# Weighted sum of two expert outputs: another row layout in HBM, hand-placed waits, and two VectorE instructions per tile

## The chip, the cores and the metric

The kernel runs on one core of one Trainium2 chip. The metric is the device time in microseconds (us) of one execution. The time before the change is 241.46 us, the median of 13 runs that lie between 241.12 and 242.02.

## The reference

A mixture-of-experts layer has sent each token to two experts, and the two results are combined with two weights per token. There are 16 x 1024 = 16384 tokens, two results of 512 float32 numbers for each, and 16384 x 2 weights.

```python
def reference(expert_outputs, combine_weights):      # (16,1024,2,512), (16,1024,2)
    weights = combine_weights[..., np.newaxis]
    return np.sum(expert_outputs * weights, axis=2).astype(np.float32)   # (16,1024,512)
```

67.1 MB are read and 33.5 MB are written; there are three arithmetic operations per output number.

## The kernel before, in words

The tokens are numbered through, and partition p of the 128 holds the 128 tokens from 128 p on. In HBM a partition's inputs are then 512 KB apart, its outputs 256 KB, and its weights 1 KB. The loop over `g` takes J = 8 tokens of every partition at a time, so there are 16 tiles. A tile is one load of 4 MB (32 KB in each partition, one contiguous run), one store of 2 MB (16 KB in each partition), and arithmetic between them.

Loads are issued by SyncE (L48) into `et`, which has four buffers; stores are issued by ScalarE (L66) from `ot`, which has four buffers too. The table of weights `wt` is one load of 128 KB, issued by ScalarE at the start (L43). A tile framework adds the semaphores: a load waits until VectorE has read the tile that used its buffer four tiles before; VectorE waits for the load, for the table, and for the store that used its output buffer four tiles before.

For each token i of the eight, VectorE runs two instructions. L57 multiplies the first expert's 512 numbers by the first weight into `ot`. L58 multiplies the second expert's 512 numbers by the second weight and adds what is in `ot`. The weight is a number per partition. These are 16 instructions a tile, on 128 x 512 elements each.

The last tile differs: the first product is made by ScalarE (L55, an activation that copies with a scale), and the store is cut in three, of 4, 2 and 2 tokens, each issued by ScalarE after its tokens are done. The first activation of a program needs a function table, which ScalarE loads in an instruction of its own.

All transfers run on the same 16 DMA engines. In the profile q1 is the queue that SyncE issues to, q10 the one that ScalarE issues to, and q14 carries instructions.

Of the kernel before, what the change touches and what calls it, by code (L numbers as in the profile page):

```python
# [1 line left out]

# [4 lines left out]


@with_exitstack
def kernel(  # L10
    ctx: ExitStack,
    tc: tile.TileContext,
    expert_outputs: bass.AP,
    combine_weights: bass.AP,
    out: bass.AP,
):


    nc = tc.nc
    b, s, k, h = expert_outputs.shape  # L20
    assert k == 2
    n = b * s
    P = nc.NUM_PARTITIONS
    per = n // P
    assert per * P == n
    eo = expert_outputs.rearrange("b s k h -> (b s) (k h)").rearrange("(p t) f -> p t f", p=P)
    cw = combine_weights.rearrange("b s k -> (b s) k").rearrange("(p t) k -> p (t k)", p=P)
    o = out.rearrange("b s h -> (b s) h").rearrange("(p t) f -> p t f", p=P)

    dt = mybir.dt.float32  # L30
    mult = mybir.AluOpType.mult
    add = mybir.AluOpType.add

    J = 8
    copy = mybir.ActivationFunctionType.Copy
    last = per // J - 1

    wpool = ctx.enter_context(tc.tile_pool(name="w", bufs=1))
    ipool = ctx.enter_context(tc.tile_pool(name="in", bufs=4))
    opool = ctx.enter_context(tc.tile_pool(name="out", bufs=4))  # L40

    wt = wpool.tile([P, per * k], dt)
    nc.scalar.dma_start(out=wt, in_=cw)  # L43

    for g in range(per // J):
        et = ipool.tile([P, J, k * h], dt)
        ot = opool.tile([P, J, h], dt)
        nc.sync.dma_start(out=et, in_=eo[:, g * J : (g + 1) * J, :])  # L48
        c0 = 0
        for c in (4, 2, 2) if g == last else (J,):  # L50
            for i in range(c0, c0 + c):
                t = g * J + i
                w0, w1 = wt[:, 2 * t : 2 * t + 1], wt[:, 2 * t + 1 : 2 * t + 2]
                if g == last:
                    nc.scalar.activation(out=ot[:, i, :], in_=et[:, i, 0:h], func=copy, scale=w0)  # L55
                else:
                    nc.vector.tensor_scalar_mul(out=ot[:, i, :], in0=et[:, i, 0:h], scalar1=w0)  # L57
                nc.vector.scalar_tensor_tensor(  # L58
                    out=ot[:, i, :],
                    in0=et[:, i, h : 2 * h],  # L60
                    scalar=w1,
                    in1=ot[:, i, :],
                    op0=mult,
                    op1=add,
                )
            nc.scalar.dma_start(  # L66
                out=o[:, g * J + c0 : g * J + c0 + c, :], in_=ot[:, c0 : c0 + c, :]
            )
            c0 += c


# [1 line left out]
_INS = ['expert_outputs', 'combine_weights']  # L73
_OUTS = [((16, 1024, 512), 'float32')]


# [23 lines left out]
```

## Time and profile before

| what | value |
|---|---|
| median of 13 runs | 241.46 us (241.12 to 242.02) |
| the profiled execution: time, span | 241.86 us, 240.1 us |
| DMA: mean rate over the span | 420 GB/s |
| HBM read, written | 67.24 MB, 33.55 MB |
| VectorE busy | 133.8 us (56%) |
| ScalarE busy | 6.4 us (3%) |
| first VectorE instruction | at 13.90 us |
| last store issued | at 236.53 us, landed 2.6 us later |

The span is the time from the first to the last instruction of the profiled execution. The time of that execution is 1.76 us longer than its span, for what lies around it. The profile is one execution, and it is 0.40 us above the median of the runs. "Landing" of a DMA is the moment its last semaphore signal arrives. In the page the DMA strip gives the busy share of the 16 DMA engines in 40 slices of 6.0 us each.

### The profile page before, as it was taken

The numbers are of one execution on the slowest core, as the hardware profiler recorded it, in microseconds if no ns is written. First come the engines' busy times: TensorE is split into PE (matmuls) and PEld (weight loads), VectorE is DVE, ScalarE is ACT, GpSimd is POOL, SyncE is SP. The second block draws the span as 40 slices with busy tenths as digits, with TensorE's granted clock in tenths as the row PEclk, the third lists the DMA queues.
The fourth block names the chain that finished last, engine by engine and source line by source line (L and its number), as shares of the span: only waits on it lengthen the run. The fifth ranks groups of instructions, "written<-read, shape, count | busy, mean of one in ns | idle before, by whom it ended". The sixth has DMA issues, their size and how long they took to land.

```text
span 240.1 us, 377 instructions
## 1 busy us (share of the span) xinstructions
DVE 133.8 (56%) x248; ACT 6.4 (3%) x9; POOL 0.2 (0%) x4
## 2 busy tenths in 40 slices
DVE  0068937629185490945819276391853918549062
ACT  0000000000000000000000000000000000000072
POOL 0000000000000000000000000000000000000000
DMA  7999999999999999999999999999999999999967
GB/s 268 439 434 431 388 407 459 414 420 459 426 429 434 442 407 431 453 418 448 442 426 426 426 437 426 423 453 437 435 437 415 431 426 442 420 442 439 412 289 306
DMA packets 5042, 100.81 MB, mean 420 GB/s; under 512 B 560, under 2 KB 688, under 8 KB 944
## 3 DMA queue, kind: packets, MB, share of 16 engines
q1 hardware_dynamic: 2304, 67.11, 65.3%
q10 hardware_dynamic: 2736, 33.69, 32.9%
q14 instruction: 2, 0.02, 0.0%
HBM read 67.24 MB, written 33.55 MB: 420 GB/s over the span
## 4 chain that ended last, share of the span: by engine, by line
DMA 56%; DVE 26%; another core or an unknown queue 13%; issue 1%; ACT 1%; SPq 0%; ACTq 0%; DVEq 0%
DMA et<-in_expert_outputs_dram 56%; DVE ot L58 16%; DVE ot L57 10%; ACT ot L55 1%; ACT L55 1%; SPq L48 0%; ACTq L66 0%; DVEq L95 0%; DVEq L57 0%; ACTq L55 0%
## 5 line engine op out<-in xcount | busy, mean ns | idle before, releaser
L57 DVE TENSOR_SCALAR ot<-et,wt 128x512 f32<-128x512 f32 x120 | 52.6, 480 | 93.4 <-DMA et<-in_expert_outputs_dram 79.5
L58 DVE SCALAR_TENSOR_TENSOR ot<-et,wt,ot 128x512 f32<-128x512 f32 x128 | 89.9, 745 | 9.3 <-ACT ot L55 9.3
L55 ACT ACT_TABLE_LOAD x1 | 1.3, 1283 | 227.8 <-DMA out_dram<-ot 227.8
L55 ACT ACTIVATE ot<-et,wt 128x512 f32<-128x512 f32 x8 | 5.1, 709 | 1.5 <-DVE ot L58 1.5
L84 POOL MEMSET const-bfloat16-1.0<- 128x1 bf16 x1 | 0.1, 103 | 0.0
L84 POOL MEMSET const-uint8-127<- 128x1 uint8 x1 | 0.1, 102 | 0.0
L84 POOL MEMSET const-float32-0.0<- 128x1 f32 x1 | 0.1, 100 | 0.2 <-issue 0.2
L84 POOL MEMSET const-float32-1.0<- 128x1 f32 x1 | 0.1, 99 | 0.0
## 6 DMA issues: line engine op xcount, KB each, us to landing
et<-in_expert_outputs_dram SPq DMA_DIRECT2D x16, 4096.0 KB, 49.5
out_dram<-ot ACTq DMA_DIRECT2D x15, 2048.0 KB, 24.8
out_dram<-ot ACTq DMA_DIRECT2D x1, 1024.0 KB, 3.9
out_dram<-ot ACTq DMA_DIRECT2D x2, 512.0 KB, 3.2
wt<-in_combine_weights_dram ACTq DMA_DIRECT2D x1, 128.0 KB, 13.1
```

What stands on the lines that cost most here:

```text
L55: nc.scalar.activation(out=ot[:, i, :], in_=et[:, i, 0:h], func=copy, scale=w0)
L57: nc.vector.tensor_scalar_mul(out=ot[:, i, :], in0=et[:, i, 0:h], scalar1=w0)
L58: nc.vector.scalar_tensor_tensor(out=ot[:, i, :], in0=et[:, i, h : 2 * h], scalar=w1, in1=ot[:, i, :], op0=mult, op1=add,)
L84: nc = _bacc.Bacc("TRN2", target_bir_lowering=False, num_devices=1)
```

## The change

Five things change together.

- The rows. The first 15360 tokens are dealt out 120 to a partition; the last 1024 tokens are a tile of their own, 8 to a partition. For the first 15 tiles a partition's inputs are then 480 KB apart in HBM and its outputs 240 KB. For the last tile they are 32 KB and 16 KB apart. The size of the runs that a DMA moves stays the same. The table of weights is loaded by two DMAs, of 240 and of 16 numbers per partition.
- The semaphores. They are placed by hand in one block. SyncE issues all loads in order. From the fifth on, a load waits for VectorE to have finished with the tile four before, as it did, and also for that tile's store to have landed. VectorE waits for both DMAs of the table, and then for each tile's load; it no longer waits for stores.
- VectorE's work on the first 15 tiles. One instruction multiplies the whole tile, 8192 numbers per partition, in place by its 16 weights, each repeated 512 times. A second one adds the two halves of each token, 4096 numbers per partition, into `ot`.
- ScalarE runs a one-element activation at its start, ahead of the two loads of the table. Its function table is loaded there.
- The last tile. ScalarE's product is written in place; VectorE's instruction is the same as L58. The store is cut in four, of two tokens each, and SyncE issues them.

The number of instructions on VectorE falls from 248 to 38. The number of DMAs and their bytes stay nearly the same.

```diff
@@ rows
-    eo = expert_outputs.rearrange("b s k h -> (b s) (k h)").rearrange("(p t) f -> p t f", p=P)
+    main = per - J
+    def rows(x):
+        a = x[0 : P * main, :].rearrange("(p t) f -> p t f", p=P)
+        b = x[P * main : n, :].rearrange("(p t) f -> p t f", p=P)
+        return lambda t, c: a[:, t : t + c, :] if t < main else b[:, t - main : t - main + c, :]
+    eo = rows(expert_outputs.rearrange("b s k h -> (b s) (k h)"))
...
@@ loads
-        nc.sync.dma_start(out=et, in_=eo[:, g * J : (g + 1) * J, :])
+    made = [2 * (g + 1) for g in range(G - 1)]
+        for g in range(G):
+            if g >= NOUT:
+                nc.sync.wait_ge(stored[g % NOUT], 16 * (g // NOUT))
+            ins = nc.sync.dma_start(out=et[:, g % NIN], in_=eo(g * J, J).rearrange("p j (k h) -> p j k h", k=k))
+            if g >= NIN:
+                ins._wait_ge(vec, made[g - NIN])
+            ins.then_inc(loaded[g], 16)
@@ table and stores
-    nc.scalar.dma_start(out=wt, in_=cw)
+        nc.scalar.activation(out=warm, in_=one, func=copy)
+        for t, c in ((0, main), (main, J)):
+            nc.scalar.dma_start(out=wt[:, t : t + c], in_=cw(t, c)).then_inc(weights, 16)
+        for g in range(G - 1):
+            nc.scalar.dma_start(out=o(g * J, J), in_=ot[:, g % NOUT])._wait_ge(
+                vec, made[g]).then_inc(stored[g % NOUT], 16)
@@ VectorE, first 15 tiles
-                    nc.vector.tensor_scalar_mul(out=ot[:, i, :], in0=et[:, i, 0:h], scalar1=w0)
-                nc.vector.scalar_tensor_tensor(out=ot[:, i, :], in0=et[:, i, h : 2 * h], scalar=w1,
-                    in1=ot[:, i, :], op0=mult, op1=add)
+        nc.vector.wait_ge(weights, 32)
+        for g in range(G - 1):
+            ek = et[:, g % NIN].rearrange("p j k h -> p (j k) h")
+            wb = wt[:, g * J : (g + 1) * J].rearrange("p j k -> p (j k)").unsqueeze(2)
+            nc.vector.tensor_tensor(out=ek, in0=ek, in1=wb.to_broadcast([P, J * k, h]), op=mult
+            )._wait_ge(loaded[g], 16).then_inc(vec, 1)
+            e = et[:, g % NIN]
+            nc.vector.tensor_tensor(out=ot[:, g % NOUT], in0=e[:, :, 0], in1=e[:, :, 1], op=add
+            )._wait_ge(vec, made[g] - 1).then_inc(vec, 1)
@@ last tile
-        for c in (4, 2, 2) if g == last else (J,):
+        for i in range(J):
...
+            if i % PIECE == PIECE - 1:          # PIECE = 2
+                f = i + 1 - PIECE
+                nc.sync.dma_start(out=o(g * J + f, PIECE), in_=ot[:, g % NOUT, f : i + 1]
+                )._wait_ge(vec, made[g - 1] + i + 1).then_inc(tail, 16)
```

More of the change, by code (lines that the diff above doesn't have):

```diff
@@ L25 @@
     assert per * P == n
-    eo = expert_outputs.rearrange("b s k h -> (b s) (k h)").rearrange("(p t) f -> p t f", p=P)
-    cw = combine_weights.rearrange("b s k -> (b s) k").rearrange("(p t) k -> p (t k)", p=P)
-    o = out.rearrange("b s h -> (b s) h").rearrange("(p t) f -> p t f", p=P)
+    J = 8
+    NIN = NOUT = 4
+    G = per // J
+    main = per - J
[4 more added lines that the diff above has]
+    eo = rows(expert_outputs.rearrange("b s k h -> (b s) (k h)"))
+    cw = rows(combine_weights.rearrange("b s k -> (b s) k"))
+    o = rows(out.rearrange("b s h -> (b s) h"))
     dt = mybir.dt.float32
@@ L32 @@
     add = mybir.AluOpType.add
-    J = 8
     copy = mybir.ActivationFunctionType.Copy
[L36 to L42, printed above, removed]
-    nc.scalar.dma_start(out=wt, in_=cw)
[L45 to L49, printed above, removed]
-        for c in (4, 2, 2) if g == last else (J,):
[L51 to L69, printed above, removed]
@@ new lines @@
+    pool = ctx.enter_context(tc.tile_pool(name="sbuf", bufs=1))
+    wt = pool.tile([P, per, k], dt)
+    warm = pool.tile([P, 1], dt)
+    et = pool.tile([P, NIN, J, k, h], dt)
+    ot = pool.tile([P, NOUT, J, h], dt)
+    loaded = [nc.alloc_semaphore(f"loaded{g}") for g in range(G)]
+    stored = [nc.alloc_semaphore(f"stored{i}") for i in range(NOUT)]
+    weights = nc.alloc_semaphore("weights")
+    tail = nc.alloc_semaphore("tail")
+    vec = nc.alloc_semaphore("vec")
+    act = nc.alloc_semaphore("act")
@@ new lines @@
+    one = nc.const_aps.tensor(1.0, (P, 1), dt)
+    PIECE = 2
+    made = [2 * (g + 1) for g in range(G - 1)]
+    with tc.tile_critical():
+        for g in range(G):
[10 more added lines that the diff above has]
+            nc.scalar.dma_start(out=o(g * J, J), in_=ot[:, g % NOUT])._wait_ge(
+                vec, made[g]
+            ).then_inc(stored[g % NOUT], 16)
+        nc.vector.wait_ge(weights, 32)
+        for g in range(G - 1):
+            ek = et[:, g % NIN].rearrange("p j k h -> p (j k) h")
+            wb = wt[:, g * J : (g + 1) * J].rearrange("p j k -> p (j k)").unsqueeze(2)
+            nc.vector.tensor_tensor(
+                out=ek, in0=ek, in1=wb.to_broadcast([P, J * k, h]), op=mult
+            )._wait_ge(loaded[g], 16).then_inc(vec, 1)
+            e = et[:, g % NIN]
+            nc.vector.tensor_tensor(
+                out=ot[:, g % NOUT], in0=e[:, :, 0], in1=e[:, :, 1], op=add
+            )._wait_ge(vec, made[g] - 1).then_inc(vec, 1)
+        g = G - 1
+        nc.scalar.wait_ge(weights, 32)
+        for i in range(J):
+            e, r = et[:, g % NIN, i], ot[:, g % NOUT, i]
+            w = wt[:, g * J + i]
+            ins = nc.scalar.activation(out=e[:, 0], in_=e[:, 0], func=copy, scale=w[:, 0:1])
+            if i == 0:
+                ins._wait_ge(loaded[g], 16)
+            ins.then_inc(act, 1)
+            nc.vector.scalar_tensor_tensor(
+                out=r, in0=e[:, 1], scalar=w[:, 1:2], in1=e[:, 0], op0=mult, op1=add
+            )._wait_ge(act, i + 1).then_inc(vec, 1)
+            if i % PIECE == PIECE - 1:
+                f = i + 1 - PIECE
+                nc.sync.dma_start(
+                    out=o(g * J + f, PIECE), in_=ot[:, g % NOUT, f : i + 1]
+                )._wait_ge(vec, made[g - 1] + i + 1).then_inc(tail, 16)
+        for i in range(NOUT):
+            nc.sync.wait_ge(stored[i], 16 * len(range(i, G - 1, NOUT)))
+        nc.sync.wait_ge(tail, 16 * (J // PIECE))
```

## The prediction

> **What bounds the kernel now.** I read the page first, then the busy time by stretches, the groups, the DMA issues, the waits of SyncE's queue and the timeline. The page's engine line, DMA strip and queue rows:
> ```profile
> DVE 133.8 (56%) x248; ACT 6.4 (3%) x9; POOL 0.2 (0%) x4
> DMA  7999999999999999999999999999999999999967
> DMA packets 5042, 100.81 MB, mean 420 GB/s; under 512 B 560, under 2 KB 688, under 8 KB 944
> q1 hardware_dynamic: 2304, 67.11, 65.3%
> q10 hardware_dynamic: 2736, 33.69, 32.9%
> q14 instruction: 2, 0.02, 0.0%
> ```
> The 16 DMA engines are full but for the first and the last slices; VectorE is busy 56%. Queue q1 holds the loads: 16 tiles x 128 rows of 32 KB are 2048 packets, and 16 signals per tile make 2304. 65.3% of 240.1 us is 156.8 us on each engine, over 128 rows: 1.22 us a row, 9.7 us a tile. A store of half the bytes is 4.85 us. The table is 688 - 560 = 128 packets, one a partition row.
>
> Busy time by stretches (us; DVE, ACT, POOL; clock; DMA share; GB/s):
> ```profile
> 4.00:14.00 10.00, 0.10 (x1) 0.00 (x0) 0.00 (x0) 1.00 1.01 432
> 24.00:38.00 14.00, 8.49 (x17) 0.00 (x0) 0.00 (x0) 1.00 0.99 406
> 125.00:154.00 29.00, 17.11 (x32) 0.00 (x0) 0.00 (x0) 1.00 1.01 433
> 228.00:232.00 4.00, 2.16 (x4) 3.99 (x6) 0.00 (x0) 1.00 0.85 365
> 232.00:236.00 4.00, 2.83 (x5) 2.21 (x4) 0.00 (x0) 1.00 0.66 271
> 236.00:240.00 4.00, 0.49 (x1) 0.00 (x0) 0.00 (x0) 1.00 0.65 261
> ```
> 432 to 433 GB/s is the same for loads alone and for loads with stores. So the middle is bound by bytes, 14.55 us a tile, and only idle DMA time can be won or lost. The one weak full stretch is 24 to 38. The idle is at the end: 0.15 x 4 + 0.34 x 4 + 0.35 x 4 = 3.4 us, of which some 1.3 us follow the last data.
>
> VectorE's two groups, then the two DMA issues that matter:
> ```profile
> L57 DVE TENSOR_SCALAR ot<-et,wt 128x512 f32<-128x512 f32 x120 | 52.6, 480 | 93.4 <-DMA et<-in_expert_outputs_dram 79.5
> L58 DVE SCALAR_TENSOR_TENSOR ot<-et,wt,ot 128x512 f32<-128x512 f32 x128 | 89.9, 745 | 9.3 <-ACT ot L55 9.3
> ```
> ```profile
> et<-in_expert_outputs_dram SPq DMA_DIRECT2D x16, 4096.0 KB, 49.5
> wt<-in_combine_weights_dram ACTq DMA_DIRECT2D x1, 128.0 KB, 13.1
> ```
> A 128 KB table that lands after 13.1 us, as late as the first tile of 4 MB (13.0 in the trace), says that each of its rows waits for a 32 KB row of the other queue. The waits of SyncE's queue:
> ```profile
> SPq L48 <- DVE ot L58: 102.8, 12, 8.6
> ```
> Today a load waits for VectorE alone. The timeline at tiles 11 to 13, and at the end:
> ```profile
> 168.73 0.88 DVE L57 TENSOR_SCALAR ot<-et,wt 128x512 f32<-128x512 f32 x2 [6.05 <-DMA et<-in_expert_outputs_dram]
> 184.14 0.88 DVE L57 TENSOR_SCALAR ot<-et,wt 128x512 f32<-128x512 f32 x2 [6.86 <-DMA et<-in_expert_outputs_dram]
> 198.69 0.88 DVE L57 TENSOR_SCALAR ot<-et,wt 128x512 f32<-128x512 f32 x2 [5.99 <-DMA et<-in_expert_outputs_dram]
> 227.79 1.28 ACT L55 ACT_TABLE_LOAD   x1 [227.79 <-DMA out_dram<-ot]
> 232.62 1.66 ACTq L66 DMA_DIRECT2D out_dram<-ot  x2
> 236.53 0.34 ACTq L66 DMA_DIRECT2D out_dram<-ot  x1
> ```
> One step is 15.41 us instead of 14.55, beside one of the two instruction fetches of q14. At the end ScalarE loads its table only when the last tile is there, and stands 1.46 us behind its own store issue.
>
> **The change part by part.** Sums go against the profiled execution: span 240.1, time 241.86, 0.40 above the median 241.46; I add the difference to the median.
>
> *VectorE.* A tile's 16 instructions become two, of 8192 and 4096 elements, both with two tensor inputs. The timeline gives starts 0.397 us apart for L57 and 0.661 for L58. From below: all elements at L57's pace, 24 x 0.397 = 9.5 us. From above: 24 pieces at L58's pace, 15.9 us. I take a fixed part and a slope: if L57 takes half a cycle per element and L58 a whole one, 745 - 480 = 265 ns are 256 cycles, so 1.035 ns per element and 0.215 us fixed; 8192 then cost 8.69, 4096 cost 4.45, together 13.2 us with the wait between them (now 8.5). That is under 14.55, so the DMA still hides it in the middle. The Trainium skill ("VectorE: DVE Perf Modes", the perf-mode tier table) says that a two-tensor fp32 instruction has no doubled mode, which speaks against this part; by its fit (N + 151)/0.96 ns a tile would be 13.1 us.
>
> *Table.* It is now two DMAs, of 960 and of 64 bytes a row, and VectorE waits for both. They are 8 + 8 rows on each engine, each behind a 32 KB row: the first lands with tile 0 (13.8), the second with tile 1. Tile 1 lands at 23.4 now; so VectorE starts at about 24.0 instead of 13.9. The eight more rows cost about 0.05 each, 0.4 us. ScalarE's function table (1.28 us) goes ahead of these issues, but their first row waits for a 32 KB row anyway: nothing.
>
> *Stores and loads.* VectorE ends tile 0 at 37.2 (before 22.4), and store 0 starts there. Load 4 now waits also for store 0 to have landed; all later loads of SyncE, and behind them the last stores, stand behind such waits. Work on hand: four loads to 13.7 + 3 x 9.7 + 0.4 = 43.2, plus store 0, 4.85: data until 48.0. The smallest store shows what a hand-over costs: 512 KB are 1.2 us of data and land 2.6 us after issue, so 1.4, and 0.2 for the issue. Load 4's data start at 49.6: the DMA idles 1.6 us. VectorE ends tile 1 at 50.4; load 4 and store 1 are 14.55 us, to 64.1. VectorE ends tile 2 at 63.6, its data at 64.6: 0.5 us idle, 0.7 with the engines' spread. Next, load 5 and store 2 reach 79.2 and store 3 is queued from 76.8: no gap, nor later, since every load finds the next store queued. Together +2.3 us; bounds 0 (VectorE near 9.5 us a tile) and 4.
>
> *End.* No table load there, no ScalarE behind its store issues: from landing to last piece 0.73 + 8 x 0.68 = 6.2 us instead of 8.8. But VectorE's longer tile puts store 14 just ahead of the last tile, so the DMA has some 10 us of stores left then: what counts is that its idle goes, 3.4 less the 1.3 after the last data: -2.1 us. This is covered as long as VectorE keeps pace.
>
> *Fewer instructions.* The late step of 15.41 should not come again: 0 to -0.9, taken -0.6, as only the last engine counts. *Added blocks* at both ends, with waits between engines: the nearest rows are SyncE's waits of 0.1 to 0.7 us at start and end; +0.5.
>
> *Pitch.* Loads and stores move from 512 and 256 KB between partitions to 480 and 240. The row of 432 to 433 GB/s leaves nothing in the middle. Bounds: 406 instead of 432 over 24 to 38 is 0.84 us, and the first rows of a cold start at most 0.6 more: -1.4 to 0, and as much against if the new pitch is worse. I take 0, as the steady rows are nearest. The Trainium skill ("DMA: Bandwidth & Descriptors", Latency and other measured facts) has a copy at 512 KB row pitch at 207 GB/s each way against 214 padded; by that, 3% or some 7 us would go and the time be near 234. The trace's 433 against the same table's 428 in sum says that this kernel does not pay it.
>
> Sum: -2.1 + 2.3 + 0.4 + 0.5 - 0.6 = +0.5 us: 242.0. What a measurement of this kernel tells from no change is about 0.2%, 0.5 us.
>
> **Rivals.**
> 1. *The pitch pays: faster.* The weak stretch at 24 to 38 and the cold first rows come from engines reading at one pitch in step; at 480 KB both go, and restarts after the two gaps are clean. Price -1.4, and -0.3 more from the instruction fetch: 240.3. It decides once it is worth over 1 us. For it: DMA share 0.99 at 406 GB/s, so packets were slow, not missing. Against: 432 from 4 to 14, at the same pitch with loads alone.
> 2. *VectorE becomes the bound: slower by much.* Its chain: 24.0 + 15 x D + 0.4 + 6.2 + 2.6 for the last piece = 33.2 + 15 D. The DMA's last landing is near 239.4, so it decides from D = 13.7, and each 0.1 us beyond costs 1.5. D = 14.5 gives about 253, the upper bound 15.9 about 274. Against: 13.2 follows from two rows that agree on one slope.
> 3. *The pitch does nothing* is the forecast itself.
>
> **How the numbers follow.** Forecast 0.52 (own range 241.0 to 243.2, of it 0.19 within 0.2%, 0.31 above, 0.02 below); the pitch 0.34, all faster; VectorE 0.14, all slower. So faster 0.36, same 0.19, slower 0.45. The range goes from 239.6 (rival 1 with the gaps nearly shut) to 245.6 (D near 14.2); about 0.18 lies outside.
>
> **What would show it.** Two VectorE groups near 8.7 and 4.5 us; first product near 24 us, waiting for the table; dents in the DMA strip near 48 and 64 us and a full strip at the end; the steady stretch still 432 to 433. Wrong would be: a table at 14 us (rows do not alternate), VectorE without waits for loads at the end and a DMA below 1.0 (rival 2), 24 to 38 at 432 with a shorter start (rival 1), or a steady rate above 435, which no step here allows.

## The result, and the profile after

The changed kernel takes 244.56 us, the median of 7 runs (244.35 to 245.06), against 241.38 for the kernel before (32 runs, 241.11 to 242.02). The runs of the kernel before lie in two groups, 241.11 to 241.46 and 241.73 to 242.02, so a difference of a few tenths of a microsecond against their median says little. The ratio is 1.0131, 95% interval 1.0118 to 1.0143. That is 3.2 us slower; the forecast was 0.5 us slower, with a range up to 245.6. The profiled execution has a span of 242.8 us and a time of 244.55.

The page of the changed kernel, engine line, strips and queues:

```profile
DVE 201.4 (83%) x38; ACT 6.5 (3%) x10; POOL 0.2 (0%) x4
DMA  7999999789999999999999999999999999999996
GB/s 264 445 435 433 432 432 373 319 278 451 410 448 432 383 459 405 443 437 432 462 432 402 462 432 400 432 435 427 435 435 432 462 432 408 459 432 400 432 412 279
q1 hardware_dynamic: 2880, 69.21, 67.5%
q10 hardware_dynamic: 2448, 31.59, 30.5%
```

The instruction queue q14 has no row any more. The DMA strip is full to the end, but slices 7 to 9 (36 to 55 us) carry 373, 319 and 278 GB/s. The dent in the DMA share (7 and 8 tenths in two slices) is smaller than that in GB/s: there the engines are partly idle and partly busy with little to show for it. The same by stretches (DVE, ACT, POOL; clock; DMA share; GB/s):

```profile
24.00:38.00 14.00, 13.97 (x3) 0.00 (x0) 0.00 (x0) 1.00 0.98 421
38.00:52.00 14.00, 13.96 (x3) 0.00 (x0) 0.00 (x0) 1.00 0.90 337
52.00:66.00 14.00, 13.96 (x3) 0.00 (x0) 0.00 (x0) 1.00 0.95 393
125.00:154.00 29.00, 28.18 (x5) 0.00 (x0) 0.00 (x0) 1.00 1.00 432
236.00:240.00 4.00, 0.00 (x0) 0.00 (x0) 0.00 (x0) 1.00 1.02 416
```

By these shares, idle time from 38 to 66 us is 0.10 x 14 + 0.05 x 14 = 2.1 us. Lost bytes, in time at 432 GB/s, are 3.1 + 1.3 = 4.4 us. The view counts a packet whole in the stretch in which it starts, so it does not place the idle time exactly. The trace's records of single packets do: there is one pause, where the prediction had two. The 16 engines run dry around 47.7 us and start again around 49.7, 2.1 us in all, and from there to 215 us none is idle. What is weak from 52 to 66 is slow packets and the counting.

VectorE's groups, its first product and the first one that waits for a load, and the first of SyncE's waits:

```profile
L90 DVE TENSOR_TENSOR et<-et,wt 128x8192 f32<-128x8192 f32 x15 | 130.3, 8688 | 31.3 <-DMA wt<-in_combine_weights_dram 23.6
L94 DVE TENSOR_TENSOR ot<-et 128x4096 f32<-128x4096 f32 x15 | 66.4, 4425 | 0.5
```

```profile
23.64 8.69 DVE L90 TENSOR_TENSOR et<-et,wt 128x8192 f32<-128x8192 f32 x1 [23.64 <-DMA wt<-in_combine_weights_dram]
142.04 8.69 DVE L90 TENSOR_TENSOR et<-et,wt 128x8192 f32<-128x8192 f32 x1 [0.75 <-DMA et<-in_expert_outputs_dram]
```

```profile
SPq L70 <- DMA out_dram<-ot: 200.6, 12, 45.6
```

The two instructions last 8.69 and 4.43 us, VectorE waits 23.6 us for the table, and all 12 later loads wait for a store.

### The profile page after: what moved, and what is told of

It reads as the page before. It is cut to its first block, busy times and chain, and to the rows that moved or that the text cites. A ratio compares the mean times of both kernels' runs of the same rounds, so it can differ in the third digit from the quotient of the medians.

```text
span 242.8 us, 153 instructions
## 1 busy us (share of the span) xinstructions
DVE 201.4 (83%) x38; ACT 6.5 (3%) x10; POOL 0.2 (0%) x4
## 4 chain that ended last, share of the span: by engine, by line
DVE 51%; DMA 45%; ACT 0%; issue 0%; SPq 0%; ACTq 0%; DVEq 0%
DVE et L90 32%; DMA out_dram<-ot 19%; DMA et<-in_expert_outputs_dram 18%; DVE ot L94 16%; DMA wt<-in_combine_weights_dram 9%; DVE ot L109 2%; ACT et L105 0%; ACT L77 0%; ACTq L145 0%; SPq L70 0%; DVEq L86 0%; SPq L65 0%
## 5 line engine op out<-in xcount | busy, mean ns | idle before, releaser
L90 DVE TENSOR_TENSOR et<-et,wt 128x8192 f32<-128x8192 f32 x15 | 130.3, 8688 | 31.3 <-DMA wt<-in_combine_weights_dram 23.6
L94 DVE TENSOR_TENSOR ot<-et 128x4096 f32<-128x4096 f32 x15 | 66.4, 4425 | 0.5
L105 ACT ACTIVATE et<-et,wt 128x512 f32<-128x512 f32 x8 | 5.0, 707 | 226.9 <-DMA et<-in_expert_outputs_dram 226.9
L109 DVE SCALAR_TENSOR_TENSOR ot<-et,wt 128x512 f32<-128x512 f32 x8 | 5.4, 748 | 2.1 <-ACT et L105 2.1
## 6 DMA issues: line engine op xcount, KB each, us to landing
wt<-in_combine_weights_dram ACTq DMA_DIRECT2D x1, 120.0 KB, 12.8
wt<-in_combine_weights_dram ACTq DMA_DIRECT2D x1, 8.0 KB, 22.2
```

What stands on the lines that cost most here:

```text
L90: nc.vector.tensor_tensor(out=ek, in0=ek, in1=wb.to_broadcast([P, J * k, h]), op=mult)._wait_ge(loaded[g], 16).then_inc(vec, 1)
L94: nc.vector.tensor_tensor(out=ot[:, g % NOUT], in0=e[:, :, 0], in1=e[:, :, 1], op=add)._wait_ge(vec, made[g] - 1).then_inc(vec, 1)
L105: ins = nc.scalar.activation(out=e[:, 0], in_=e[:, 0], func=copy, scale=w[:, 0:1])
L109: nc.vector.scalar_tensor_tensor(out=r, in0=e[:, 1], scalar=w[:, 1:2], in1=e[:, 0], op0=mult, op1=add)._wait_ge(act, i + 1).then_inc(vec, 1)
```

## The experiments

Two theories stood against each other at first. G: the time is lost in pauses of the DMA (it counts two, where the packet records show one), which come from the late table together with loads that wait for stores. V: VectorE's long instructions are the cost. P was a third, that the slow rows around the pauses belong to the new pitch. A slow row is a DMA packet of 32 KB, the part of a load that goes to one partition, that takes longer than the usual 1.21 us. The pitch is the distance in HBM from one partition's data to the next one's.

**Loads no longer wait for stores.** VectorE waits for the store instead, just before the instruction that overwrites `ot`.

```diff
-            if g >= NOUT:
-                nc.sync.wait_ge(stored[g % NOUT], 16 * (g // NOUT))
             ins = nc.sync.dma_start(out=et[:, g % NIN], ...)
...
             e = et[:, g % NIN]
+            if g >= NOUT:
+                nc.vector.wait_ge(stored[g % NOUT], 16 * (g // NOUT))
             nc.vector.tensor_tensor(out=ot[:, g % NOUT], ...)
```

> The changed kernel, but a load no longer waits for the store of four tiles before; VectorE waits for that store before its second instruction instead. Theory G (the 3.2 us come from two pauses of the DMA near 48 and 64 us, and from the slow first rows after a pause; the pauses come from loads that wait for stores to land): load 4 is issued at 36.8 instead of 48.2, no pause, the 2.4 us of idle and some 1.3 to 1.9 us of slow rows go: 240.3 to 241.2. Rival P (the slow rows are the new pitch's): only the idle goes, 242.1. Rival V (VectorE's 13.1 us per tile are themselves the cost, whatever the loads wait for): 244.0 to 244.6.

Measured: 240.84 us (11 runs), ratio to before 0.9975 (0.9965 to 0.9985). The waits of SyncE's queue in this run show that loads stand behind VectorE again:

```profile
SPq L68 <- DVE ot L93: 173.6, 12, 33.7
```

V predicted 244 and falls; P predicted 242.1 and falls.

**The old rows.** `rows` returns 128 tokens per partition again; everything else, the two table DMAs too, stays.

```diff
-        a = x[0 : P * main, :].rearrange("(p t) f -> p t f", p=P)
-        b = x[P * main : n, :].rearrange("(p t) f -> p t f", p=P)
-        return lambda t, c: a[:, t : t + c, :] if t < main else b[:, t - main : t - main + c, :]
+        a = x.rearrange("(p t) f -> p t f", p=P)
+        return lambda t, c: a[:, t : t + c, :]
```

> The changed kernel with the old rows: 128 tokens per partition in a row, 512 and 256 KB apart, also in the last tile; the table still in two DMAs of 960 and 64 bytes a row. Theory G: the pauses and the slow rows stay, 244.0 to 245.0. Rival P: the slow rows after the pauses go (1.9 us), 242.6. If instead the new pitch helps, this run is slower than 245.

Measured: 246.72 us (4 runs), ratio 1.0214 (1.0197 to 1.0232). The old pitch is 2.2 us worse here, so P has the wrong sign, and G's 244 to 245 is missed too: the slow rows are there with either pitch, and the new one is cheaper. Its stretches:

```profile
38.00:52.00 14.00, 13.96 (x3) 0.00 (x0) 0.00 (x0) 1.00 0.82 309
80.00:125.00 45.00, 44.86 (x8) 0.00 (x0) 0.00 (x0) 1.00 0.99 422
```

Against the changed kernel, 38 to 52 has more idle (0.82, not 0.90), and 80 to 125 is at 422, not 434 GB/s. By the packet records the difference of the two profiled executions, 2.2 us, is 0.5 of idle in the first 5 us, 0.7 of idle around the pause and near 80 us, 0.5 of slow rows, and 0.5 because the engines end further apart.

**VectorE waits for the first table only.** The second DMA of the table gets a semaphore of its own, waited for ahead of the last tile.

```diff
-            nc.scalar.dma_start(out=wt[:, t : t + c], in_=cw(t, c)).then_inc(weights, 16)
+            nc.scalar.dma_start(out=wt[:, t : t + c], in_=cw(t, c)).then_inc(weights if t == 0 else weights2, 16)
-        nc.vector.wait_ge(weights, 32)
+        nc.vector.wait_ge(weights, 16)
...
-        nc.scalar.wait_ge(weights, 32)
+        nc.scalar.wait_ge(weights2, 16)
+        nc.vector.wait_ge(weights2, 16)
```

> The changed kernel, but VectorE waits only for the first of the table's two DMAs; the second is waited for ahead of the last tile. Theory G: VectorE starts at 13.7 instead of 23.6, store 0 goes out at 26.8 and lands before the loads run dry, no pause: 240.0 to 241.2, although VectorE's instructions are the long ones. Rival V: VectorE is 83% busy and stays the cost, 243 or more.

Measured: 240.37 us (6 runs), ratio 0.9953 (0.9940 to 0.9966): the lowest median of all, 4.2 us below the changed kernel. VectorE is as busy as there (201.8 us), with its long instructions. From this run, the timeline's first product and first stores, then the stretches where the pause was:

```profile
13.86 8.69 DVE L91 TENSOR_TENSOR et<-et,wt 128x8192 f32<-128x8192 f32 x1 [13.86 <-DMA wt<-in_combine_weights_dram]
27.04 196.90 ACTq L82 DMA_DIRECT2D out_dram<-ot  x15
```

```profile
38.00:52.00 14.00, 13.96 (x3) 0.00 (x0) 0.00 (x0) 1.00 1.01 435
52.00:66.00 14.00, 13.96 (x3) 0.00 (x0) 0.00 (x0) 1.00 1.00 431
```

Store 0 goes out at 27.0 instead of 36.8, and both stretches are full. The wait for 8 KB had opened the pause, though not by itself: without the loads' wait for stores (the first experiment) it opens none, and the next experiment shows the same for a shorter tile of VectorE. The packet records account for the whole difference of the two profiled executions, 4.3 us: 2.1 of idle in the pause, 2.0 of slow rows, and 0.2 because the engines end further apart.

**Short VectorE instructions in the changed kernel.** The pair for the whole tile is replaced by L57's and L58's kind, token by token, with the semaphore counts adapted.

```diff
-            nc.vector.tensor_tensor(out=ek, in0=ek, in1=wb.to_broadcast([P, J * k, h]), op=mult)...
-            nc.vector.tensor_tensor(out=ot[:, g % NOUT], in0=e[:, :, 0], in1=e[:, :, 1], op=add)...
+            for i in range(0, J, 2):
+                for j in (i, i + 1): nc.vector.tensor_scalar_mul(out=r[:, j], in0=e[:, j, 0], scalar1=w[:, j, 0:1])...
+                for j in (i, i + 1): nc.vector.scalar_tensor_tensor(out=r[:, j], in0=e[:, j, 1], scalar=w[:, j, 1:2], in1=r[:, j], ...)
```

> The changed kernel with VectorE's 16 short instructions per tile (8.5 us) on the first 15 tiles; the late table and the loads' wait for stores stay. Theory G: store 0 goes out at 32.2 and lands at about 48, load 4 then follows while stores 1 and 2 are still queued, so no idle, and most slow rows are gone: 240.3 to 241.5. Rival V gives the same here; a rival in which the late table alone costs the time gives 244 or more.

Measured: 241.62 us (12 runs), ratio 1.0008 (0.9999 to 1.0017). No pause, as G has it, but 1.25 us slower than the run before and 0.1 above G's range. The rival of the late table alone, 244 or more, falls. Its q14 row is back, with two packets of 8 KB. That opened a second question: what do short instructions cost?

**The new rows alone, in the kernel before.** `rows` as in the change; the table lies in two tiles, so that the first 15 tiles wait for the first DMA only.

```diff
+    wa = wpool.tile([P, main, k], dt)
+    wz = wpool.tile([P, 8, k], dt)
+    nc.scalar.dma_start(out=wa, in_=cw(0, main))
+    nc.scalar.dma_start(out=wz, in_=cw(main, 8))
-        nc.sync.dma_start(out=et, in_=eo[:, g * J : (g + 1) * J, :])
+        nc.sync.dma_start(out=et, in_=eo(g * J, J))
```

> The kernel before with the new rows alone (480 and 240 KB; the table in two tiles, so VectorE's first 15 tiles wait for the first one only). Theory G: the pitch matters where reads restart or stores first come between them, and before there are no pauses: of its 1.45 us of slow rows 0.7 are the cold start and stay, so 240.4 to 241.3. Rival P (the pitch is worth the 2.2 us of the run with the old pitch everywhere): 239.2.

Measured: 241.76 us (11 runs), ratio 1.0011 (1.0000 to 1.0021): no gain at all, and outside G's range; rival P, 239.2, falls.

**The new end alone, in the kernel before.**

```diff
+    nc.scalar.activation(out=warm, in_=nc.const_aps.tensor(1.0, (P, 1), dt), func=copy)
-        for c in (4, 2, 2) if g == last else (J,):
+        for c in (2, 2, 2, 2) if g == last else (J,):
-            nc.scalar.dma_start(
+            (nc.sync if g == last else nc.scalar).dma_start(
```

> The kernel before with the new end alone: ScalarE's function table is loaded at the start, the last tile's store is cut in four of two tokens and issued by SyncE. The prediction's term: the DMA's 2.1 us of idle at the end go, 239.3. Rival: part of the idle is the distance from the last landing to the first piece and stays, 240.0 to 240.6. A third, that the end is bound by the last product's chain alone: 1.28 + 1.46 us less, 238.7.

Measured: 241.25 us (11 runs), ratio 0.9991 (0.9981 to 1.0001). The prediction's 2.1 us were not there, and neither rival's range was met. Its end by stretches:

```profile
228.00:232.00 4.00, 4.00 (x7) 4.00 (x7) 0.00 (x0) 1.00 0.96 411
232.00:236.00 4.00, 1.31 (x2) 0.17 (x1) 0.00 (x0) 1.00 1.02 417
236.00:240.00 4.00, 0.00 (x0) 0.00 (x0) 0.00 (x0) 1.00 0.18 74
```

The idle from 228 to 236 is gone indeed (before: 0.85 and 0.66). But by the packet records, the 16 engines now send their last signals between 236.3 and 238.1 us, where before all sent them within 0.15 us. Fourteen engines end by 237.1, and two late, at 237.75 and 238.1.

**Both waits mended.** The two edits of the first and the third experiment together.

> The changed kernel with both mends, VectorE waiting for the first table only and for the stores in the loads' place. Theory G: each mend alone has removed the pauses already, so there is nothing left to gain: 240.2 to 240.6, as the better of the two. If each wait cost something of its own: 239.5 or less.

Measured: 240.65 us (7 runs), ratio 0.9968 (0.9957 to 0.9980), 0.05 above G's range. Nothing more to gain, as G has it.

**First table only, with the old rows.** The third experiment's edit on top of the second's.

> The changed kernel with VectorE waiting for the first table only (no pauses) and with the old rows. Theory G: without pauses the pitch is worth little, 240.4 to 241.2. Rival P: 2.2 us as with pauses, 242.6.

Measured: 241.02 us (12 runs), ratio 0.9985 (0.9976 to 0.9994). Without a pause the new pitch is worth 0.65 us (241.02 against 240.37), with it 2.2. The two profiled executions differ by 0.8 us: 0.4 of idle in the first 5 us, and 0.4 because the engines end further apart.

**What short instructions cost.** The edits of the third and the fourth experiment together; there is no pause in either.

> The changed kernel with VectorE waiting for the first table only, and with the 16 short VectorE instructions per tile. Neither this nor its pair with the long instructions (240.37) has a pause. Theory F (VectorE's 248 instructions need two fetches of 8 KB during the run, each of which sets one DMA engine back by nearly a microsecond, and the last engine decides): 241.1 to 241.6, with two packets on the instruction queue and the engines' last signals spread over 1 us and more. Rival: the fetches cost nothing that counts, 240.2 to 240.5.

Measured: 241.74 us (11 runs), ratio 1.0010 (1.0001 to 1.0018): 1.37 us above the same kernel with the long instructions, although VectorE is busy a third less. That is 0.1 above F's range; the rival falls. The queue row of this run:

```profile
q14 instruction: 2, 0.02, 0.0%
```

By the packet records, two fetches of 8 KB start at 45.6 and 162.8 us, and the last signals are spread from 236.6 to 238.4, against 236.5 to 236.9 with the long instructions. Each fetch takes 0.31 us, and the 32 KB row that starts as it ends takes 1.75 instead of 1.21: a delay of 0.84 us. The 16 signals of each load show it stay: they are spread over 1.55 us from the fourth to the eleventh load, and over 2.39 from the first load after the second fetch on. At the end one engine is 1.64 us later than the median of the 16. Two delays are 1.68; the records do not name the engine, so that both fell on the same one is inferred from this sum.

**VectorE's long instructions alone, in the kernel before.**

```diff
+        if g < last:
+            nc.vector.tensor_tensor(out=ek, in0=ek, in1=wb.to_broadcast([P, J * k, h]), op=mult)
+            nc.vector.tensor_tensor(out=ot, in0=et[:, :, 0:h], in1=et[:, :, h : 2 * h], op=add)
+            nc.scalar.dma_start(out=o[:, g * J : (g + 1) * J, :], in_=ot)
+            continue
```

> The kernel before with VectorE's two long instructions alone on the first 15 tiles; one table, loads that wait for VectorE alone, old rows, old end. Theory G with F: no pause, since VectorE starts at 13.8, and no fetch (-0.9); the stores come 4.6 us later, so the loads are ahead and the end has less idle: 239.6 to 240.6. Rival V (the long instructions cost time): above 241.5. No change, 241.4, if only the idle at the end decides.

Measured: 240.44 us (5 runs), ratio 0.9960 (0.9947 to 0.9973). This one part of the change brings nearly all that the best version has. It has no fetch, and the end is full without a change to it:

```profile
228.00:232.00 4.00, 2.02 (x3) 1.33 (x2) 0.00 (x0) 1.00 0.95 406
232.00:236.00 4.00, 0.00 (x0) 0.00 (x0) 0.00 (x0) 1.00 0.99 408
```

The longer tile puts stores behind loads: the timeline has the first product of the last tile at 222.5, not 229.1, and the stores then fill the end.

**New rows and new end, in the kernel before.** The edits of the two runs above, together.

> The kernel before with the new rows and the new end, and its own short VectorE instructions, waits and single wait for the first table. Theory F: the fetches stay, one engine is late and takes the gain of the closed idle at the end: 240.8 to 241.4. If the parts add up freely (pitch +0.2, idle -2.1): 239.5.

Measured: 241.33 us (11 runs), ratio 0.9996 (0.9987 to 1.0005). That is in F's range, and the parts do not add up freely.

**The fetch by itself.** The third experiment's kernel with 15 one-element activations on the idle ScalarE after each store issue.

```diff
             nc.scalar.dma_start(out=o(g * J, J), in_=ot[:, g % NOUT])...
+            for i in range(15):
+                nc.scalar.activation(out=many[:, 15 * g + i : 15 * g + i + 1], in_=one, func=copy)
```

> The changed kernel with VectorE waiting for the first table only, its two long instructions per tile, and 15 one-element activations on ScalarE after each store issue (225 in all, of no use to the output). ScalarE is idle there: 15 x 0.2 us after an issue are done long before the next. Theory F (it is the fetch of instructions by the DMA engines that costs, whatever engine they are for): two packets of 8 KB come back on the instruction queue, one DMA engine ends late, and the time goes from 240.37 to 241.1 to 241.8. Rival (the difference between long and short VectorE instructions is VectorE's own): 240.3 to 240.6.

Measured: 241.20 us (12 runs), ratio 0.9985 (0.9975 to 0.9994), 0.83 us above the kernel without the activations (0.8 by the two ratios); VectorE's work is the same in both.

```profile
q14 instruction: 2, 0.02, 0.0%
```

(In the run without them this row has one packet too, but of 32 bytes, at 0.2 us.) The fetches of 8 KB are back, at 71.9 and 185.1 us, the last signals are spread from 236.8 to 238.1, and the time has moved where the theory put it. The rows behind the two fetches take 1.46 and 1.56 us, so the delays are 0.56 and 0.65, together 1.21; one engine ends 1.25 us later than the median of the 16. The extra activations put the last tile's first product 1.1 us later (226.1 against 225.0), but the median engine ends only 0.1 us later than without them, so the late engine is the cost. So what long instructions gain in these pairs is the fetch that they avoid, not anything on VectorE. Why the row after a fetch is slow, and why it is less so here than behind VectorE's fetches, no run tells.

## Why the prediction was right, and where it was not

The direction was right, but only just: the forecast of +0.5 us was as large as what the prediction itself said a measurement can tell from no change, and 244.56 lies above the forecast's own range, which ended at 243.2. It lies in the whole range because rival 2, VectorE as the bound, stretched that to 245.6, and rival 2 did not occur; that part is luck. (By the prediction's own figures, 253 at a tile of 14.5 us and 1.5 us for each 0.1, 245.6 belongs to a tile of 14.0, not 14.2.)

Most steps were right. VectorE's tile was put at 13.2 us, and its starts are 13.06 apart; its start was put at 24.0 and is 23.64. The full strip at the end came as written, and the stretch from 125 to 154 runs at 432 GB/s. VectorE caught up with the loads at 142 us and waited for each from there on. The added blocks were put at 0.5: the first load is issued at 0.94 instead of 0.73, and the span ends some 0.3 us later after the last data. The idle was put at 2.3 us, 1.6 near 48 and 0.7 near 64, and is 2.1. That this agrees is luck too: the first pause is longer than forecast, and the second did not come.

The sum was short by 2.7 us. The third experiment cuts it in two, since it has every part of the change but the pause.

- *The pause* was priced at 2.3 us and costs 244.56 - 240.37 = 4.2, above the term's own bound of 4. The step that failed is the term "Together +2.3 us", which counts idle time alone and prices the rows after a pause like any others. That a restart could be anything but clean appears only in rival 1, and there it is tied to the pitch. The packet records show 32 KB rows of 1.21 us nearly everywhere, and many of 1.4 to 2.3 us in four places: at the start, at the first store, after the pause, and once more from 76 to 80 us. Summed per engine, rows are 3.4 us over their usual length in the changed kernel, 1.3 in the third experiment and 1.4 before. These 2.0 us are the missing ones. The row for it was on the page: the weak stretch from 24 to 38 was such a place, and the prediction used it for the pitch alone.
- *Everything else* was priced at -1.8 (-2.1 end, -0.6 fetch, +0.4 table rows, +0.5 blocks) and measures -1.0 (240.37 against 241.38, the new pitch's gain included). Here the step that failed is the end's -2.1 as a term of its own. The size of the idle was read nearly right: by the packet records the engines are idle for 1.9 us between 215 us and the last data before, and for 0.2 in the third experiment. But it is not free time as long as one engine is late: the end alone brought 0.1 us, the long instructions alone 0.9. End and fetch are one term: as long as the fetches stay, closing the end brings next to nothing. The fetch was priced at 0 to -0.9; with the end closed, it measures 0.83 and 1.37. The table rows' +0.4 was too large: a row of 64 bytes takes 0.011 us, so eight of them 0.1.

Rival 1 was wrong as a mechanism: the new pitch alone gains nothing. It was right that the pitch matters, 2.2 us with a pause and 0.65 without, but only part of the 2.2 lies around the pause. Why rows are slow after a pause, and why 512 KB between partitions costs more at the start, at the pause and in the engines' spread at the end, no run here tells.

The rule that weighed against the change, the Trainium skill's tier table in "VectorE: DVE Perf Modes", held: by that page's fit for the fp32 instruction with two tensors (its section on the TRN2 errata) a tile is 13.1 us, an estimate, and 8.69 + 4.43 were measured. The 3% that the prediction worked out from the skill's row for a 512 KB pitch ("DMA: Bandwidth & Descriptors", Latency and other measured facts) did not show in the steady stretch: the kernel before runs at 433 GB/s there, the changed one at 432.

## What to carry to other kernels

Where the DMA is the bound, ask of each wait not how long it is, but whether the queue of transfers can run dry behind it: a wait for 8 KB at the start cost 4.2 us here, although VectorE had caught up long before the end. Price a pause at its idle time and the slow rows of the restart, here about as much again. And an engine that is never the bound can still cost DMA time by its number of instructions; two long ones for sixteen short ones brought 0.9 us here, although they kept VectorE busy half as long again.

## What the hardware showed that was not expected

- With some 240 instructions on one engine (248 on VectorE, or 235 on ScalarE) the trace has two fetches of 8 KB on the instruction queue during the run; with 38 on VectorE and 10 on ScalarE it has none. A fetch takes 0.31 us of a DMA engine, and the 32 KB row that starts as it ends takes 1.75 us (1.46 and 1.56 behind ScalarE's) instead of 1.21. The kernel then ends with that one late engine: 1.37 us more with VectorE's short instructions, 0.83 with ScalarE's. The last signals are spread over 1.8 and 1.3 us instead of 0.3.
- A table whose rows are 64 bytes lands 22.2 us after its issue if it stands second in a queue beside 32 KB rows (the first, of 960 bytes, after 12.8).
- The first 32 KB rows after a pause take up to 2.3 us instead of 1.21 with 480 KB between partitions, and up to 2.2 with 512.
